# Even layer up to the output projection: the key norm's root pinned later, projections ahead of scores from the second key group on, other banks for the statistics

## The chip, the cores and the metric

The kernel runs on one core of one Trainium2 chip. Its time is the device time of one execution in microseconds (us). The figure for a kernel is the median of several executions. One further execution is taken with the hardware profiler; its spans, waits and chains are what the text argues from.

The engines are called as the profile calls them: PE is TensorE (matmul), PEld its weight loads, DVE is VectorE, ACT is ScalarE, POOL is GpSimd, and SP is the engine whose queue issues nearly all DMAs here. SBUF is the on-chip memory, PSUM the matmul's accumulation memory of eight banks.

## What is computed

The input is 1024 tokens of width 1024, with 16 meta tokens put ahead, so 1040 columns. Two layers follow. The first ("even") layer is the one that the change touches. Cut to what matters:

```python
def even_layer(z, w_in, ...):                       # z = rms_norm(h, norm_g[0])
    zp = jnp.einsum('btd,de->bte', z, w_in)
    c_q, c_kv, k_pe, q_s, k_s, v_s, gate = split_cols(zp, EVEN_SPLITS)   # 384, 256, 64, 1024, 256, 256, 2048
    y_a = mla_mixer(c_q, c_kv, k_pe, ...)           # 8 heads, full attention, low-rank q and kv
    y_b = swa_mixer(q_s, k_s, v_s, ...)             # 8 query heads, 2 key heads, window +-128 and the meta tokens, learned sink
    y = jnp.concatenate([y_a, y_b], axis=-1) * jax.nn.silu(gate)
    return jnp.einsum('bte,ed->btd', y, w_out)

def swa_mixer(q_s, k_s, v_s, g_qn, g_kn, sink, cos, sin):
    q = apply_rope(rms_norm(q, g_qn), cos, sin)     # 8 heads of 128
    k = apply_rope(rms_norm(k, g_kn), cos, sin)     # 2 heads of 128, each serves 4 query heads
    ...                                             # softmax over sink, 16 meta keys, 384 band keys; times v
```

The second ("odd") layer is a gated linear recurrence in both directions with its own projections; the change leaves it as it is. All products are of float32 accuracy: each operand is split into a high and a low part in a reduced format, and three matmuls (low by high, high by low, high by high) make one product.

## The kernel before

Activations lie transposed, 128 features on the partitions and the 1040 columns along the free axis; a projection of 128 output features is `proj1`. It has two halves of four 128-row pieces each; a half is 36 matmuls (4 pieces, 3 terms, 3 column chunks of `C3`: 348, 346, 346). Its weights come by a 256 KB load on SP's queue and are split into high and low on POOL (`split_w`, lines 106 and 107).

A Python program writes the work down in one order. A list scheduler then gives each engine its own queue: it takes instructions by priority (earlier in the program is higher, and weight loads are moved ahead), and if one is not ready by the scheduler's own reckoning it takes a later one that is. On the chip each queue is in order, so a queue that is ahead of the data simply waits. Every SBUF tile comes from a pool with a fixed number of buffers per tag (`T`, `S`, ...), every PSUM tile from a bank tag, and a new tile waits until a buffer is released.

The stages of the even layer that the change touches:

1. **Up projections** (lines 415 to 478). `uq_pair` makes three 128-row tiles of queries for two heads (the rope part first, j = 2, then j = 0 and 1), `uk_pair` two tiles of keys. `take` copies a tile out of PSUM in three chunks, on DVE or on ACT; `fold` squares it on ACT. The sums of squares over the partitions come from `stat`: POOL and DVE split the squares in two (lines 173 and 174), and the inner function `later` runs the matmuls against a column of ones and copies three chunks out on ACT (lines 188 and 189). `put_off(n, fn)` queues such a function; `tick()`, called once per finished tile, counts down and runs what has come due. PSUM has tags `b` (2 banks for each chunk) and `one` (2 banks).
2. **Window attention** (from line 515). PSUM tags: `b` 1 bank for each chunk, `s` 2, `t` 2, `a` 1. First `v_prep`, `k_prep(0)`, `q_prep(0)` and `gate_tile(0)` run. `k_prep(g)` projects the keys of key head g, starts the norm's statistic, and ropes the keys; `fin` (one tick later) runs the statistic and `row_rsqrt`: the row of sums goes to DRAM and comes back as a 16x65 tile, DVE takes the inverse root by three Newton steps (lines 126 to 132), and the result goes to DRAM again. `fin2` (two ticks later) reads it back broadcast to all partitions (`rkb`) and multiplies the keys by it (line 554). `put` splits the keys into `kh` and `kl` (lines 561 to 564). `q_prep` is alike for two query heads.
   Then 36 units follow, each two query heads by 128 queries (or the 16 meta queries, `i == 8`). A unit has `scores` (matmuls at line 684, softmax in place, last step line 703), `turn` (transposes, lines 718 and 721, tiles `tA` and `tB` of tag `t`, copied out at lines 723 to 732) and `values` (line 743, copied out as `yt`, stored to `s_yb`). Iteration c of the loop does `scores(c)`, `turn(c-1)`, `pull`, `values(c-2)`. `pull` advances a chain of the remaining projections (`q_prep(1)` to `gate_tile(9)`, 32 half-projection steps, each priced 5.3) by a credit of 4.6. Units 0 to 17 use key head 0, units 18 to 35 key head 1; at c = 18 `put` and `v_split` of key head 1 run first.
3. **The last gates** (line 822). `gate_tile(e, False)` for e = 10 to 15: projection, tanh, product (lines 766 to 769), and then `gated`: it loads the attention output `yb`, multiplies it by the gate on POOL (line 779) and splits it (lines 758 and 759). The tiles of e = 8 and 9, whose gates were stored earlier, are multiplied in the same loop. Tag `T` has 8 buffers here.
4. **The output projection's first half** (line 944) over `YH[8:16]`, with weights split on POOL again.

Of the kernel before, what the change touches and what calls it, by code (L numbers as in the profile page):

```python
# [7 lines left out]
F32 = mybir.dt.float32  # L8
# [9 lines left out]
T = 1040  # L18
# [23 lines left out]
def trunk_kernel(ctx: ExitStack, tc: tile.TileContext, a: dict, out: bass.AP):  # L42
# [126 lines left out]
    def stat(sq, s, m, dst, tag=None, rt="S"):  # L169

        hi = row("sqh", rt, F32R)
        lo = row("sql", rt, F32R)
        nc.gpsimd.tensor_scalar(hi, sq, 1.0, 1.0, ALU.mult, ALU.mult)
        nc.vector.tensor_sub(lo, sq, hi.bitcast(F32))

        def later():
            sr = row("sr", "T")
            if tag is None:
                ps = big("st")
                for j, x in enumerate((hi, lo)):  # L180
                    for c0, c1 in CH:
                        nc.tensor.matmul(ps[:m, OFF + c0:OFF + c1], s, x[:, c0:c1], start=j == 0, stop=j == 1)
                nc.scalar.copy(sr[:m], ps[:m, OFF:OFF + T])
            else:
                for c0, c1 in C3:
                    ps = bank("st", tag)
                    for j, x in enumerate((hi, lo)):
                        nc.tensor.matmul(ps[:m, :c1 - c0], s, x[:, c0:c1], start=j == 0, stop=j == 1)
                    nc.scalar.copy(sr[:m, c0:c1], ps[:m, :c1 - c0])
            nc.sync.dma_start(dst, sr[:m])  # L190

        return later
# [240 lines left out]
    def uq_pair(pr):  # L433
        for j in (2, 0, 1):
            ps = up_tile(a["uq"][pr * 3 + j], 3, cqh, cql)
            r = row("qr", "T")
            if j == 2:
                take(ps, r)
                t2 = row("qs2", "S")
                nc.scalar.activation(t2, r, AF.Square)  # L440
                rope(r, 32, tabC, tabS)
                nc.sync.dma_start(s_qr[pr], r)
                t0, t1 = row("qs0", "S"), row("qs1", "S")
            else:
                take(ps, r, True)
                fold(r, j, t0, t1)
                nc.sync.dma_start(s_qn[2 * pr + j], r)
        nc.vector.tensor_add(t0, t0, t2)
        nc.vector.tensor_add(t0, t0, t1)
        put_off(3, stat(t0, sel, 2, d_mq[pr], "one"))  # L450

    def uk_pair(pr):
        t0, t1 = row("ks0", "S"), row("ks1", "S")
# [4 lines left out]
            fold(r, j, t0, t1)  # L458
            nc.sync.dma_start(s_kn[2 * pr + j], r)
        nc.vector.tensor_add(t0, t0, t1)  # L460
        put_off(3, stat(t0, sel, 2, d_mk[2 * pr:2 * pr + 2], "one"))

    for pair, pr in ((uq_pair, 0), (uq_pair, 1), (uk_pair, 0), (uq_pair, 2), (uk_pair, 1), (uk_pair, 2), (uk_pair, 3),
                     (uq_pair, 3)):
# [72 lines left out]
    def k_prep(g):  # L537
# [7 lines left out]
        sk = stat(sq, one, 1, d_sk[g], "s")  # L545
        rope(raw, 64, sC, sS, eng=nc.gpsimd)

        def fin():
            sk()
            row_rsqrt(d_sk[g], 128, d_rks[g])  # L550

        def fin2():
            rkb = bcast_row(d_rks[g], "rkb", "T")
# [11 lines left out]
            KV[g, "k"] = (kh.rearrange("p b c -> p (b c)"), kl.rearrange("p b c -> p (b c)"))  # L565

        put_off(1, fin)
        put_off(2, fin2)
        KV[g, "put"] = put
        yield 5.3  # L570
# [184 lines left out]
    def split(src, nm, tag, w=T, eng=nc.vector):  # L755
# [3 lines left out]
        eng.tensor_sub(lo[:, :w], src[:, :w], hi[:, :w].bitcast(F32))  # L759
        return hi, lo  # L760

    def gate_tile(e, spill=True):
        o = []
        yield from steps(proj1(16 + e), o)
        g = row("gt", "T")
        evac(o[0], lambda t, c: nc.vector.scalar_tensor_tensor(g[:, c], t, 0.5, rstd[:, c], ALU.mult, ALU.mult))
# [3 lines left out]
        if spill:  # L770
            nc.sync.dma_start(s_gate[e], t)
        else:
            gated(e, t)
        yield 5.3

    def gated(e, t):
        y = row("yb", "T")
        nc.sync.dma_start(y, s_yb[e - 8])
        nc.gpsimd.tensor_mul(y, y, t)
        YH[e], YL[e] = split(y, "yb", "Y")  # L780

    def chain(*gs):
# [22 lines left out]
    for c in range(n + 2):  # L805
        if c < n:
            if units[c].i == 8:
                flush()
                if c == 18:
                    KV[1, "put"]()  # L810
                    v_split(1, None)
            units[c].scores()
        if 0 <= c - 1 < n:
            units[c - 1].turn()
        pull(jobs, PULL)
        if 0 <= c - 2 < n:
            units[c - 2].values()
    for _ in jobs:
# [4 lines left out]
    for e in range(8 + NX, 16):  # L823
        for _ in gate_tile(e, False):
            pass
        if e - 8 - NX < NX:
            t = row("gl", "T")
            nc.sync.dma_start(t, s_gate[e - NX])
            gated(e - NX, t)

    HD = {}
    LAG = 2.0
# [672 lines left out]
```

## Time and profile before

| what | value |
|---|---|
| median of 3 executions | 1940.13 us (1939.22 to 1945.82) |
| the profiled execution | 1936.07 us |
| its span, first to last instruction | 1934.3 us |
| mean granted TensorE clock | 0.986 of full |
| PE busy | 1828.5 us (95%) |
| DVE busy | 1278.4 us (66%) |
| POOL busy | 943.9 us (49%) |
| ACT busy | 827.9 us (43%) |
| stages: up projections | about 100 to 197 us of the span |
| window attention with projections | about 197 to 594 us |
| last gates | about 594 to 662 us |
| output projection, first half | from 666 us |

Times in the rows of a timeline are microseconds from the span's start. "idle before <-releaser" in brackets is the time that the engine had nothing to do before this instruction, and the instruction or DMA that ended it. Waits for PE are what costs time, as PE is busy nearly throughout; a wait of another engine matters only where PE comes to wait for what it was to make. In a row of stretches ("windows"), each engine has its busy time and count, then the granted TensorE clock, the DMA engines' busy share and GB/s.

### The profile page before, as it was taken

The numbers are of one execution on the slowest core, as the hardware profiler recorded it, in microseconds if no ns is written. First come the engines' busy times: TensorE is split into PE (matmuls) and PEld (weight loads), VectorE is DVE, ScalarE is ACT, GpSimd is POOL, SyncE is SP. The second block draws the span as 40 slices with busy tenths as digits, with TensorE's granted clock in tenths as the row PEclk, the third lists the DMA queues.
The fourth block names the chain that finished last, engine by engine and source line by source line (L and its number), as shares of the span: only waits on it lengthen the run. The fifth ranks groups of instructions, "written<-read, shape, count | busy, mean of one in ns | idle before, by whom it ended". The sixth has DMA issues, their size and how long they took to land.

```text
span 1934.3 us, 28455 instructions
## 1 busy us (share of the span) xinstructions
PE 1828.5 (95%) x10822; PEld 1659.4 (86%) x10822; DVE 1278.4 (66%) x1953; ACT 827.9 (43%) x1366; POOL 943.9 (49%) x780
## 2 busy tenths in 40 slices
PE   8999989998999999999999999999999899988999
PEld 7988988888999999788878999988888788876887
DVE  7686358787663432889888753368898989893000
ACT  5455224444342201666666642155656464652000
POOL 5455355535224652544433333358676777655331
PEclk9999999999999999999999999999999999998999
DMA  5256532222223451323221014312222222246521
GB/s 180 73 184 232 132 84 65 64 75 72 78 75 122 143 194 57 113 73 92 69 70 55 18 47 160 106 50 71 82 67 81 84 69 88 66 157 232 183 82 44
DMA packets 111062, 192.77 MB, mean 100 GB/s; under 512 B 32143, under 2 KB 51727, under 8 KB 110926
## 3 DMA queue, kind: packets, MB, share of 16 engines
q1 hardware_dynamic: 110926, 190.96, 31.4%
q8 instruction: 85, 1.39, 0.3%
q14 instruction: 51, 0.42, 0.1%
HBM read 129.86 MB, written 53.06 MB: 95 GB/s over the span
## 4 chain that ended last, share of the span: by engine, by line
PE 53%; DVE 20%; POOL 9%; issue 9%; DMA 5%; ACT 4%; SPq 1%; DVEq 0%; ACTq 0%; POOLq 0%
PE pj L159 10%; PE oo L159 8%; PE pxop L159 6%; PE px L918 4%; PE av L998 4%; PE op L159 3%; PE up L159 3%; PE tp L982 3%; PE vps L426 2%; DVE tz L1243 2%; DMA wr<-in_wg 2%; POOL oz L1253 2%; POOL wl L107 2%; DVE oxc L1167 2%; PE pg L1143 2%
## 5 line engine op out<-in xcount | busy, mean ns | idle before, releaser
L106 POOL TENSOR_SCALAR wh<-wr 128x512 fp32r<-128x512 f32 (+2 forms) x219 | 196.3, 897 | 396.4 <-PE pj L159 99.0
L107 POOL TENSOR_TENSOR wl<-wr,wh 128x512 fp32r<-128x512 f32 (+2 forms) x219 | 352.6, 1610 | 17.5
L159 PE MATMUL pj<-xh,wl 128*128 128x346 f32 (+1 forms) x768 | 251.8, 328 | 12.3 <-DVE wl L107 7.2
L159 PE MATMUL pj<-xl,wh 128*128 128x346 f32 (+1 forms) x768 | 249.3, 325 | 0.7 <-DVE xl L260 0.6
L159 PE MATMUL pj<-xh,wh 128*128 128x346 f32 (+1 forms) x768 | 248.9, 324 | 0.0
L159 PEld LDWEIGHTS pj<-xh,wl 128*128 128x128 f32 x768 | 146.6, 191 | 14.2 <-ACT xh L259 7.1
L159 PEld LDWEIGHTS pj<-xl,wh 128*128 128x128 f32 x768 | 146.7, 191 | 2.2 <-DVE xl L260 2.1
L159 PEld LDWEIGHTS pj<-xh,wh 128*128 128x128 f32 x768 | 146.6, 191 | 0.1
L936 POOL TENSOR_SCALAR mpm<-p,mmx 128x96 f32<-128x96 f32 (+1 forms) x69 | 25.7, 372 | 209.2 <-DVE mmx L931 119.9
L1143 PE MATMUL pu<-h1h,wl 128*128 128x346 f32 (+1 forms) x384 | 125.5, 327 | 0.8 <-POOL wh L106 0.8
L1143 PE MATMUL pu<-h1l,wh 128*128 128x346 f32 (+1 forms) x384 | 124.9, 325 | 0.0
L1143 PE MATMUL pu<-h1h,wh 128*128 128x346 f32 (+1 forms) x384 | 124.8, 325 | 0.0
L988 ACT CAST pth<-tp 128x512 fp32r<-128x512 f32 (+1 forms) x160 | 78.9, 506 | 83.4 <-PE tp L982 82.0
L1294 DVE TENSOR_TENSOR hres<-oo,hres 128x512 f32<-128x512 f32 x16 | 10.6, 687 | 151.6 <-PE oo L159 151.6
L989 DVE TENSOR_TENSOR ptl<-tp,pth 128x512 fp32r<-128x512 f32 (+1 forms) x160 | 91.9, 583 | 23.3 <-ACT pth L988 21.7
L159 PE MATMUL oo<-oyl,wh 128*128 128x512 f32 x256 | 102.3, 400 | 4.4 <-DMA oyl<-s_yl 4.4
L159 PE MATMUL oo<-oyh,wl 128*128 128x512 f32 x256 | 100.3, 401 | 3.3 <-DMA oyh<-s_y 3.3
L159 PE MATMUL oo<-oyh,wh 128*128 128x512 f32 x256 | 102.7, 402 | 0.0
L1143 PE MATMUL pg<-h1h,wl 128*128 128x512 f32 x256 | 101.4, 396 | 0.0
L1143 PE MATMUL pg<-h1h,wh 128*128 128x512 f32 x256 | 101.1, 395 | 0.0
L1143 PE MATMUL pg<-h1l,wh 128*128 128x512 f32 x256 | 100.8, 394 | 0.0
L982 PE MATMUL tp<-ident,p 128*128 128x128 f32 (+1 forms) x576 | 96.2, 274 | 0.0
(446 smaller groups left out, 5564.5 us busy)
## 6 DMA issues: line engine op xcount, KB each, us to landing
wr<-in_w SPq DMA_DIRECT2D x128, 256.0 KB
wr<-in_wo SPq DMA_DIRECT2D x64, 256.0 KB
s_y<-oyh SPq DMA_DIRECT2D x14, 512.0 KB
s_yl<-oyl SPq DMA_DIRECT2D x14, 512.0 KB
oyh<-s_y SPq DMA_DIRECT2D x14, 512.0 KB
oyl<-s_yl SPq DMA_DIRECT2D x14, 512.0 KB
s_g<-gth SPq DMA_DIRECT2D x10, 520.0 KB
xr<-in_x SPq DMA_DIRECT2D x8, 520.0 KB
```

The lines of the kernel that those rows point to most:

```text
L106: eng.tensor_scalar(hi[:, :n], raw[:, :n], 1.0, 1.0, ALU.mult, ALU.mult)
L107: eng.tensor_sub(lo[:, :n], raw[:, :n], hi[:, :n].bitcast(F32))
L159: nc.tensor.matmul(t[:, :c1 - c0], w, x[:, c0:c1], start=first and j == 0 and pi == 0, stop=last and j == nt - 1 and pi == 2)
L426: nc.tensor.matmul(ps[:m, :n], s, w, start=j == 0 and pi == 0, stop=j == nt - 1 and pi == 2)
L918: nc.tensor.matmul(dst[:m, d0:d0 + a1 - a0], l[:, s], r[:, a0:a1], start=pi == 0, stop=pi == 4)
L982: nc.tensor.transpose(tp[:, o:o + m], p_[:m, NM + P * (kt + j):NM + P * (kt + j) + P], ident[:m, :m])
L988: nc.scalar.copy(hi[:, :w], tp[:, :w])
L989: nc.vector.tensor_sub(lo[:, :w], tp[:, :w], hi[:, :w].bitcast(F32))
L998: nc.tensor.matmul(av[:, :n], l[:, vs], pts[kt][o][:, j * n:j * n + n], start=kt == 0 and j == 0 and pi == 0, stop=False)
L1143: nc.tensor.matmul(t[:, :c1 - c0], l, r[:, c0:c1], start=hf == 0 and k == 0 and pi == 0, stop=hf == 1 and k == 3 and pi == 2)
L1167: nc.vector.scalar_tensor_tensor(xc[:, 2:T], u[:, 0:T - 2], cw[0], xc[:, 2:T], ALU.mult, ALU.add)
L1243: nc.vector.scalar_tensor_tensor(tz[:, d, :n], av[:, :n], 1.0, tz[:, d, :n], ALU.add, ALU.mult)
```

## The change

Seven edits, all in the even layer up to the output projection:

- `stat` with tag `s` puts its third chunk into a bank of tag `t`.
- `uq_pair` copies the tile j = 1 out on ACT in place of DVE.
- The statistics of `uq_pair` and `uk_pair` are put off four ticks in place of three.
- In `k_prep`, `fin` only runs the statistic and loads the row back; the root and its store move to a new `fin1`, one tick later, just ahead of `fin2`. The root's first instruction is pinned behind the DVE instruction that was written last before it (an order on the queue, no wait for its result).
- In `gate_tile(e, False)` and for e = 8 and 9 the load of `yb` is written ahead of the projection (or of the product).
- The product `yb` times gate moves from POOL to DVE.
- From c = 18 on, `pull` comes ahead of `scores(c)`; iterations 36 and 37 keep it where it was.

```diff
@@ -182,8 +182,8 @@
                         nc.tensor.matmul(ps[:m, OFF + c0:OFF + c1], s, x[:, c0:c1], start=j == 0, stop=j == 1)
                 nc.scalar.copy(sr[:m], ps[:m, OFF:OFF + T])
             else:
-                for c0, c1 in C3:
-                    ps = bank("st", tag)
+                for c, (c0, c1) in enumerate(C3):
+                    ps = bank("st", "t" if tag == "s" and c == 2 else tag)
                     for j, x in enumerate((hi, lo)):
                         nc.tensor.matmul(ps[:m, :c1 - c0], s, x[:, c0:c1], start=j == 0, stop=j == 1)
                     nc.scalar.copy(sr[:m, c0:c1], ps[:m, :c1 - c0])
@@ -442,12 +442,12 @@
                 nc.sync.dma_start(s_qr[pr], r)
                 t0, t1 = row("qs0", "S"), row("qs1", "S")
             else:
-                take(ps, r, True)
+                take(ps, r, j == 0)
                 fold(r, j, t0, t1)
                 nc.sync.dma_start(s_qn[2 * pr + j], r)
         nc.vector.tensor_add(t0, t0, t2)
         nc.vector.tensor_add(t0, t0, t1)
-        put_off(3, stat(t0, sel, 2, d_mq[pr], "one"))
+        put_off(4, stat(t0, sel, 2, d_mq[pr], "one"))
 
     def uk_pair(pr):
         t0, t1 = row("ks0", "S"), row("ks1", "S")
@@ -458,7 +458,7 @@
             fold(r, j, t0, t1)
             nc.sync.dma_start(s_kn[2 * pr + j], r)
         nc.vector.tensor_add(t0, t0, t1)
-        put_off(3, stat(t0, sel, 2, d_mk[2 * pr:2 * pr + 2], "one"))
+        put_off(4, stat(t0, sel, 2, d_mk[2 * pr:2 * pr + 2], "one"))
 
     for pair, pr in ((uq_pair, 0), (uq_pair, 1), (uk_pair, 0), (uq_pair, 2), (uk_pair, 1), (uk_pair, 2), (uk_pair, 3),
                      (uq_pair, 3)):
@@ -545,9 +545,19 @@
         sk = stat(sq, one, 1, d_sk[g], "s")
         rope(raw, 64, sC, sS, eng=nc.gpsimd)
 
+        got = []
+
         def fin():
             sk()
-            row_rsqrt(d_sk[g], 128, d_rks[g])
+            t16 = small.tile([16, 65], F32, tag="t16", name="t16", bufs=2)
+            nc.sync.dma_start(t16, flat(d_sk[g]))
+            got.append(t16)
+
+        def fin1():
+            t16 = got[0]
+            tc.keep_in_program_order(nc.vector.scalar_tensor_tensor(t16, t16, 1.0 / 128, e16, ALU.mult, ALU.add))
+            y16 = newton_rsqrt(t16, [16, 65], "16")
+            nc.sync.dma_start(flat(d_rks[g]), y16)
 
         def fin2():
             rkb = bcast_row(d_rks[g], "rkb", "T")
@@ -565,6 +575,7 @@
             KV[g, "k"] = (kh.rearrange("p b c -> p (b c)"), kl.rearrange("p b c -> p (b c)"))
 
         put_off(1, fin)
+        put_off(2, fin1)
         put_off(2, fin2)
         KV[g, "put"] = put
         yield 5.3
@@ -759,8 +770,15 @@
         eng.tensor_sub(lo[:, :w], src[:, :w], hi[:, :w].bitcast(F32))
         return hi, lo
 
+    def y_in(e):
+        y = row("yb", "T")
+        nc.sync.dma_start(y, s_yb[e - 8])
+        return y
+
     def gate_tile(e, spill=True):
         o = []
+        if not spill:
+            y = y_in(e)
         yield from steps(proj1(16 + e), o)
         g = row("gt", "T")
         evac(o[0], lambda t, c: nc.vector.scalar_tensor_tensor(g[:, c], t, 0.5, rstd[:, c], ALU.mult, ALU.mult))
@@ -770,13 +788,11 @@
         if spill:
             nc.sync.dma_start(s_gate[e], t)
         else:
-            gated(e, t)
+            gated(e, t, y)
         yield 5.3
 
-    def gated(e, t):
-        y = row("yb", "T")
-        nc.sync.dma_start(y, s_yb[e - 8])
-        nc.gpsimd.tensor_mul(y, y, t)
+    def gated(e, t, y):
+        nc.vector.tensor_mul(y, y, t)
         YH[e], YL[e] = split(y, "yb", "Y")
 
     def chain(*gs):
@@ -809,10 +825,13 @@
                 if c == 18:
                     KV[1, "put"]()
                     v_split(1, None)
+            if c >= 18:
+                pull(jobs, PULL)
             units[c].scores()
         if 0 <= c - 1 < n:
             units[c - 1].turn()
-        pull(jobs, PULL)
+        if c < 18 or c >= n:
+            pull(jobs, PULL)
         if 0 <= c - 2 < n:
             units[c - 2].values()
     for _ in jobs:
@@ -826,7 +845,7 @@
         if e - 8 - NX < NX:
             t = row("gl", "T")
             nc.sync.dma_start(t, s_gate[e - NX])
-            gated(e - NX, t)
+            gated(e - NX, t, y_in(e - NX))
 
     HD = {}
     LAG = 2.0
```

## The prediction

> **What bounds the kernel.** I read the page's busy times first, then PE's waits up to 260 us and from 260 to 700 us (columns: total us, times, longest), then a row of stretches around the longest of them.
>
> ```profile
> PE 1828.5 (95%) x10822; PEld 1659.4 (86%) x10822; DVE 1278.4 (66%) x1953; ACT 827.9 (43%) x1366; POOL 943.9 (49%) x780
> ```
>
> ```profile
> PE st L188 <- DVE sql L174: 3.8, 3, 1.7
> ```
>
> ```profile
> PE tA L718 <- DVE sp L703: 7.3, 10, 1.6
> PE st L188 <- ACT sr L189: 6.0, 5, 1.9
> PE pj L159 <- ACT qraw L318: 3.9, 1, 3.9
> PE pxop L159 <- POOL wh L106: 3.2, 1, 3.2
> PE sps L684 <- DVE kl L564: 2.9, 1, 2.9
> PE sps L684 <- ACT kh L562: 1.1, 1, 1.1
> ```
>
> ```profile
> 248.00:282.00 34.00, 29.37 (x166) 27.73 (x165) 23.20 (x30) 12.15 (x21) 19.06 (x14) 0.90 0.30 81
> 436.00:450.00 14.00, 10.09 (x51) 9.71 (x50) 7.31 (x17) 5.38 (x12) 5.16 (x7) 0.76 0.36 104
> 594.00:662.00 68.00, 67.54 (x428) 67.54 (x429) 25.81 (x28) 12.80 (x14) 40.43 (x28) 1.00 0.34 117
> 662.00:672.00 10.00, 6.78 (x28) 6.53 (x27) 4.58 (x6) 2.72 (x3) 6.60 (x5) 0.66 0.73 243
> ```
>
> PE is busy for 95% of the span, so no other engine's work counts unless PE waits for it. All that the change can win lies in PE's idle time: 3.8 + 7.3 + 6.0 + 3.9 + 3.2 + 2.9 + 1.1 = 28.2 us in these rows, and the 7.3 us of transposes waiting for the softmax are not addressed by any edit. That leaves 20.9 us.
>
> The stretches show a second price. The granted clock is 0.90, 0.76 and 0.66 in the three that hold the three longest stops, and 1.00 in the one between. PE's timeline shows what that costs:
>
> ```profile
> 263.95 0.66 PE L159 MATMUL pj<-xh,wl 128*128 128x348 f32 x1 [3.93 <-ACT qraw L318]
> 268.94 0.32 PE L159 MATMUL pj<-xh,wh 128*128 128x346 f32 x1
> 269.89 0.32 PE L159 MATMUL pj<-xh,wh 128*128 128x346 f32 x1
> 666.02 0.63 PE L159 MATMUL pxop<-ybh,wl 128*128 128x348 f32 x1 [3.22 <-POOL wh L106]
> 671.63 0.32 PE L159 MATMUL pxop<-ybl,wh 128*128 128x346 f32 x1
> ```
>
> From 263.95 to 268.94 PE starts 17 matmuls, 0.29 us apart; from 268.94 to 269.89 six, 0.158 apart. At 0.158 the 17 would take 2.7 us, so the slow stretch costs 2.3 us. From 666.02 to 671.63 there are 19, 5.6 us for 3.0: it costs 2.6. The third stretch I price alike at 2.5, an estimate from these two. So the stops of 3.93, 1.1 + 2.9 and 3.22 us cost another 7.4 us together, and the whole that the edits can reach is 20.9 + 7.4 = 28.3 us.
>
> **The change part by part.** All positions are those of the profiled execution.
>
> *The root of key head 0.* DVE, then ACT:
>
> ```profile
> 254.28 0.22 DVE L313 SCALAR_TENSOR_TENSOR t<-t,e 16x65 f32<-16x65 f32 x1 [6.34 <-DMA t<-d_sk]
> 258.26 0.22 DVE L132 SCALAR_TENSOR_TENSOR nw_y<-nw_t,nw_y 16x65 f32<-16x65 f32 x1
> 258.40 1.22 DVE L398 TENSOR_TENSOR sw<-sw,sS 128x1040 f32<-128x1040 f32 x1
> 260.81 1.53 DVE L400 TENSOR_TENSOR qraw<-qraw,sw 128x1040 f32<-128x1040 f32 x1
> 262.38 1.06 ACT L624 CAST sqh__2740<-qraw 128x1040 fp32r<-128x1040 f32 x1 [10.95 <-DVE qraw L400]
> 263.45 1.14 ACT L318 COPY qraw<-pj 128x348 f32<-128x348 f32 x3
> ```
>
> DVE stood 6.34 us for the row that comes back from DRAM, then made the root (254.28 to 258.48, 4.2 us), then the query's rope (258.40 to 262.34, three operations, 3.9 us). ACT's split of that query waits for the rope and stands ahead of the next evacuation (263.45), for which PE waits until 263.95. With the root one tick later and pinned, the rope goes first. It can't start before its swapped copy has landed, which no row shows; the bounds are the 4.2 us of the root that leave its front plus the wait, and nothing. I take the middle of 0 and 4.2, some 2.2 us. PE's stop falls from 3.9 to 1.7 us, too short for a slow stretch by the rows seen here, so 2.2 + 2.3 = **4.5 us** (bounds 0 and 6.2). The root itself, the DRAM round trip and the split of the keys come later; they are covered by the gate's projection, 72 matmuls or 11.4 us. If that cover is too short, the first scores wait for the keys.
>
> *Statistics put off by four ticks; one copy on ACT.* The 3.8 us of `st L188 <- DVE sql L174` are three statistics whose low part DVE had not finished when PE came to them. One more tile of work (18 matmuls for keys, 27 for queries, so 2.8 us at least at 0.158) stands in between now, and the longest wait was 1.7. Three chunk copies for each of four query pairs leave DVE, the late engine, for ACT. Against it: the split squares stay in their buffers one tile longer, with six buffers of that tag, and a later fold may wait. I take **3.8 us** (bounds 1.5 and 4.5).
>
> *The third chunk in a bank of tag t.* The 6.0 us are the third chunk waiting for ACT to empty the first of only two banks.
>
> ```profile
> 410.84 0.68 DVE L727 TENSOR_TENSOR pl<-tA,ph 128x512 fp32r<-128x512 f32 x1
> 413.00 0.32 PE L188 MATMUL st<-sqh,ones 128*1 128x346 f32 x1 [1.90 <-ACT sr L189]
> ```
>
> At 413.00 the longest, 1.90 us. Its new bank holds the transposes that DVE reads until 410.84 + 0.68 = 411.52, so about 0.5 us of wait stay there, a gain of 1.4. The other 4.1 us go, but the next transposes find one of their two banks held until ACT's last chunk copy; for that I take off 1.5. Together **4.0 us** (bounds 1.5 and 6.0).
>
> *Projections ahead of scores.* In the steady state the order scores, turn, pull, values becomes pull, scores, turn, values. Between a unit's scores and its own turn lie one pull, one set of values and the next scores in both, so the 7.3 us stay. Two places differ. The first is unit 18:
>
> ```profile
> 425.15 0.22 DVE L132 SCALAR_TENSOR_TENSOR nw_y<-nw_t,nw_y 16x65 f32<-16x65 f32 x1
> 429.08 0.38 SPq L143 DMA_DIRECT2D rkb<-d_rks  x1
> 434.44 1.24 DVE L554 TENSOR_TENSOR kraw<-kraw,rkb 128x1040 f32<-128x1040 f32 x1 [2.44 <-DMA rkb<-d_rks]
> 435.78 0.42 DVE L732 TENSOR_TENSOR spmr<-tB,spmr 32x256 fp32r<-32x256 f32 x1
> 439.07 1.35 DVE L564 TENSOR_TENSOR kl<-kraw,kh 128x128 fp32r<-128x128 f32 x1
> ```
>
> Here the root ended at 425.37, the row was back on all partitions at 434.44, and the low keys were ready at 440.42; PE had stopped for 1.1 and 2.9 us. A half projection of 36 matmuls, 5.7 us, would now come first and hide it. But the root of this head moves as well. It is pinned behind the last instruction of the turn of unit 16, line 732, here at 435.78, or 433.3 without the 2.44 us of waiting just ahead of it. So it ends at 433.3 + 4.2 = 437.5. The round trip took 434.44 - 425.37 = 9.1 us here, 3.7 of them before SP issued the load at 429.08; with 8 us the row is back at 445.5, and 4 to 6 us later, at 449.5 to 451.5, the keys are ready. PE's two stops before 440.42 began at some 436.3, where the values of unit 15 ended; the step would run from there to 442.0. The root's store and the load back stand on SP's queue behind whatever weight load waits for POOL, which is how the 3.7 us came about. If the scores are next on its queue it stops for 8 us where it stopped for 4 (a loss of 4); if the scheduler fills with the turn, the values and the next step (2 + 5.7 us, to 449.7), almost nothing is left (a gain of 3.9 + 2.5 = 6.4). It fills by its own reckoning, and that reckoning took the keys for ready 4 us too early here. I take a stop of 3 us with its slow stretch: **1.0 us**.
>
> The second place is the end. The 32 steps run out at the 36th pull (36 x 4.6 / 5.3 = 31.2), which was the cover of the last softmax and now stands ahead of its scores:
>
> ```profile
> 581.83 0.30 PE L684 MATMUL sps<-kh,sqh__5194 128*128 128x288 f32 x1
> 582.75 0.41 PE L159 MATMUL pj<-xh,wl 128*128 128x348 f32 x1
> 588.52 0.28 PE L743 MATMUL av<-pl,svh 128*128 128x256 f32 x1
> 594.46 0.43 PE L159 MATMUL pj<-xh,wl 128*128 128x348 f32 x1 [0.74 <-ACT yt L746]
> 585.54 0.71 DVE L703 TENSOR_SCALAR sp<-sp,ssm 128x272 f32<-128x272 f32 x2
> 592.49 0.42 DVE L732 TENSOR_TENSOR spmr<-tB,spmr 32x256 fp32r<-32x256 f32 x1
> ```
>
> The last scores ended at 582.13 and the next stage began at 594.46, 12.3 us of which the step took 582.75 to 588.52, 5.8. Without it 6.6 remain. The softmax needs until 586.25, 4.1 us after the scores. The last turn and its copies took from about 589.7 (ten matmuls of values after 588.52) to 592.91, 3.2 us, and the last values with their copy 1.55. In a chain that is 4.1 + 3.2 + 1.55 = 8.9 us for 6.6: I take **-2.5 us** (bounds 0, if the next stage's projection could start sooner, which the wait for `yt` at 594.46 speaks against, and -5 with a slow stretch).
>
> *The last gates.* POOL splits the weights and also multiplied the tiles:
>
> ```profile
> L779 POOL TENSOR_TENSOR yb<-yb,gth 128x1040 f32<-128x1040 f32 x6 | 14.6, 2426 | 18.2 <-DVE gth L769 12.7 <-DMA yb<-s_yb 5.5
> L779 POOL TENSOR_TENSOR yb<-yb,gl 128x1040 f32<-128x1040 f32 x2 | 6.9, 3446 | 0.0
> L759 DVE TENSOR_TENSOR ybl<-yb,ybh 128x1040 fp32r<-128x1040 f32 x8 | 15.1, 1892 | 29.5 <-ACT ybh L758 29.5
> ```
>
> Eight products, 14.6 + 6.9 = 21.5 us, leave POOL, which was busy 40 of 68 us. The last splits for the output projection were queued behind the product of tile 14 and came 3.22 us late. DVE takes over eight operations like its line 759, at most 1.9 us each, 15 us; it was busy 25.8 of 68 us, and the product now follows the gate on the same engine with no POOL between. The loads of `yb` are issued sooner on SP's queue. If POOL was the last to be late, 3.2 + 2.6 = **5.8 us** (bounds 2 and 5.8).
>
> The sum is 4.5 + 3.8 + 4.0 + 1.0 - 2.5 + 5.8 = 16.6 us. The profiled execution took 1936.07, so its like takes 1919.5. The median was 4.1 us above it, at 1940.13, so I say **1923.5**.
>
> The slow stretches have a page. The Trainium skill, "TensorE: Matmul & The Clock Gate", section "HAM oscillation — how this bites in real kernels", says that the clock falls back after idle gaps of over some 3.4 us. Here stops of 3.22 us, and of 3.14 in a stage not touched, were followed by a lower clock too, so the trace draws the line lower:
>
> ```profile
> 974.77 0.38 PE L918 MATMUL py<-knh,qnl 128*128 128x256 f32 x1 [3.14 <-ACT p L928]
> ```
>
> By the page's figure a stop of 3 us at unit 18 would keep full speed, and the sum would be 19.1 us; by the rows it may lose it, as I have counted.
>
> **The rivals.** *The waits come back elsewhere.* In-order queues that were late for one reason are late for the next: DVE stands for the key rows ahead of the softmaxes (the row at 434.44 shows such a stand), unit 18 stops for 8 us (-4 for +1, 5 us less) and the bank swap is paid back in the turns (4 us less). That leaves 7.6 us, 1932.5 by the median. For it: the 7.3 us of softmax waits show how little slack DVE has. Against it: DVE's load falls.
>
> *All of it is covered.* Unit 18 has its keys in time (+6.4) and the tail costs nothing: 16.6 + 5.4 + 2.5 = 24.5 us, 1915.6.
>
> *The other side: the load of `yb` holds up SP's queue.* It stands ahead of a projection's weights, takes one of eight `T` buffers, and if none is free all weights behind it wait until the tile before is split. The price per tile is what late weights cost at 666.02, 3.22 + 2.6 = 5.8 us; six tiles are 35 us against the other parts' 10.8 us, so 1964. It decides from the second such tile on. Against it: a tile needs three buffers at a time, five where a stored gate is loaded, and weight loads have their own priority ahead.
>
> **How the numbers follow.** The forecast, gains of 11 to 24 us, has 0.53; covered in full 0.11; the waits come back 0.24; SP's queue 0.05; the other 0.07 is a schedule that shifts in later stages, split between same and slower. What a measurement of this kernel can tell from no change is about 0.5%, 9.7 us either way. All of the first two, 0.64, is faster; the third is just under 9.7 and goes to same, with 0.03 of the rest: 0.27; slower 0.09. The range runs from 1910 (the bounds of all terms, 28 us) to 1938 (the returned waits with the tail at its worst, and the scatter of the runs).
>
> **What would show it.** In the changed profile: no waits of `st` for `sql` before 160 us; waits of `st` for `sr` under 2 us in all; the stop at some 260 us under 2 us and the clock 1.00 up to 430 us; a stop of 2 to 4 us ahead of the scores of unit 18; 2 to 3 us more idle around the last turn; no stop ahead of the first `pxop`, and POOL's busy time 21 us lower with DVE's some 10 to 15 higher. The forecast is wrong if PE's idle time up to 680 us falls by under 8 us, or if a new stop of over 4 us appears there.

## The result, and the profile after

The changed kernel is slower: 1959.44 us median (1949.19 to 1962.53) against 1939.84 us for the kernel before on the same chip, a ratio of 1.0095 with a 95% interval of 1.0074 to 1.0116. The forecast was 1923.5 us, range 1910 to 1938. The profiled execution took 1959.94 us, its span 1958.1, 23.8 us more than before. By the medians it is 19.6 us: the profiled execution of the kernel before was 3.8 us under its median.

Engine totals of the changed kernel, then its PE waits up to 260 us, then those from 260 to 700 us (columns: total us, times, longest):

```profile
PE 1836.9 (94%) x10822; PEld 1665.0 (85%) x10822; DVE 1285.5 (66%) x1949; ACT 832.9 (43%) x1378; POOL 922.6 (47%) x772
```

```profile
PE st L188 <- ACT sr L189: 2.1, 3, 0.9
PE st L188 <- DVE sql L174: 2.0, 1, 2.0
PE up L159 <- DVE kr L318: 1.3, 1, 1.3
```

```profile
PE st L188 <- DVE sql L174: 8.7, 1, 8.7
PE tA L729 <- DVE sp L714: 8.0, 12, 1.6
PE sps L695 <- DVE qm L638: 4.7, 1, 4.7
PE sps L695 <- ACT kh L572: 3.1, 1, 3.1
PE sps L695 <- ACT sr L189: 2.6, 3, 1.4
PE sps L695 <- DVE kl L574: 2.4, 1, 2.4
PE pj L159 <- ACT qraw L318: 2.4, 1, 2.4
...
PE pxop L159 <- POOL wh L106: 0.8, 1, 0.8
```

The waits that the edits aimed at did shrink (`pj` for `qraw` 3.9 to 2.4, `pxop` 3.2 to 0.8, the 6.0 us of `st` for `sr` in the attention gone). But there are two new ones of 8.7 and 4.7 us, and they hang on DVE. Where the 23.8 us arose, from the first matmul of each stage in PE's timeline:

| first matmul of | before, us | after, us | behind |
|---|---|---|---|
| values' projection | 197.46 | 200.57 | 3.1 |
| first scores | 281.97 | 292.53 | 10.6 |
| scores of unit 9 | 356.92 | 371.48 | 14.6 |
| projections behind the attention | 594.46 | 614.73 | 20.3 |
| output projection (`pxop`) | 666.02 | 687.18 | 21.2 |
| end of the span | 1934.3 | 1958.1 | 23.8 |

The largest steps are the first scores (7.5 us), the stretch from unit 9 to the projections behind the attention (5.7 us) and the nine units behind the first scores (4.0 us). The last of these goes with a slow clock, as the rows of stretches show, whose last three numbers are the granted clock, the share of DMA and GB/s: 0.96 from 282 to 436 us, where before it was 1.00. Cut finer it is 0.75 from 292 to 300 us, right behind the two stops, and 1.00 from 300 us on. 0.94 and 0.92 stand at the two ends of the table, ahead of the values' projection and behind the attention.

```profile
110.00:170.00 60.00, 54.99 (x328) 51.15 (x327) 40.19 (x50) 38.92 (x55) 36.66 (x34) 0.94 0.53 182
248.00:282.00 34.00, 26.23 (x163) 24.80 (x162) 15.22 (x19) 8.64 (x15) 18.14 (x15) 1.00 0.30 76
282.00:436.00 154.00, 135.48 (x864) 127.06 (x864) 116.14 (x275) 67.31 (x180) 68.50 (x71) 0.96 0.25 62
594.00:662.00 68.00, 64.49 (x393) 63.15 (x392) 36.12 (x58) 16.89 (x32) 22.89 (x22) 0.92 0.32 107
```

How the two stops came about is read from DVE's timeline and SP's of the changed kernel (start, duration, and in brackets the idle time before with what ended it):

```profile
260.50 1.24 DVE L398 TENSOR_TENSOR sw<-sw,sS 128x1040 f32<-128x1040 f32 x1 [9.59 <-DMA sw<-qraw]
...
267.10 0.21 DVE L558 SCALAR_TENSOR_TENSOR t<-t,e 16x65 f32<-16x65 f32 x1
...
274.07 1.35 DVE L132 SCALAR_TENSOR_TENSOR nw_y<-nw_t,nw_y 16x65 f32<-16x65 f32 x1
281.41 1.24 DVE L564 TENSOR_TENSOR kraw<-kraw,rkb 128x1040 f32<-128x1040 f32 x1 [5.99 <-DMA rkb<-d_rks]
...
284.91 1.23 DVE L174 TENSOR_TENSOR sql<-qs,sqh 128x1040 fp32r<-128x1040 f32 x1
...
286.26 1.24 DVE L398 TENSOR_TENSOR sw<-sw,sS 128x1040 f32<-128x1040 f32 x1
...
292.21 0.17 DVE L638 TENSOR_TENSOR qm<-qraw,qm 128x16 fp32r<-128x16 f32 x1
```

```profile
275.45 0.33 SPq L560 DMA_DIRECT2D d_rks<-nw_y  x1
276.80 0.33 SPq L143 DMA_DIRECT2D rkb<-d_rks  x1
277.23 0.47 SPq L396 DMA_DIRECT2D sw<-qraw  x1
```

DVE's first rope operation had to wait 9.59 us for the swapped copy, and the pinned root behind it began at 267.10 in place of 254.28, though the load of its row had been issued at 255.57 (in the kernel before DVE began the root 2.1 us after that issue). It took 8.3 us (to 275.42) where it took 4.2. SP stood 9.1 us for the root (the row of its waits says `SPq L560 <- DVE nw_y L132: 9.1, 1, 9.1`) and could issue the second query's swap only behind it, at 277.23. DVE then stood 5.99 us for the row of roots, and behind that stood the low part `sql` of the query's squares, for which PE stopped 8.67 us, and the second query's rope and split, for which it stopped 4.73 us.

### The profile page after: what moved, and what is told of

The parts are those of the page before. It is cut to its first block, busy times and chain, and to the rows that moved or that the text cites. A ratio compares the mean times of both kernels' runs of the same rounds, so it can differ in the third digit from the quotient of the medians.

```text
span 1958.1 us, 28468 instructions
## 1 busy us (share of the span) xinstructions
PE 1836.9 (94%) x10822; PEld 1665.0 (85%) x10822; DVE 1285.5 (66%) x1949; ACT 832.9 (43%) x1378; POOL 922.6 (47%) x772
## 4 chain that ended last, share of the span: by engine, by line
PE 48%; DVE 16%; POOL 6%; issue 5%; DMA 3%; ACT 3%; SPq 0%; DVEq 0%; ACTq 0%; POOLq 0%
PE pj L159 9%; PE oo L159 8%; PE pxop L159 6%; PE px L937 4%; PE av L1017 4%; PE op L159 3%; PE tp L1001 3%; PE pg L1162 3%; PE pu L1162 2%; DVE tz L1262 2%; DMA wr<-in_wg 2%; PE py L937 2%; POOL oz L1272 2%; DVE oxc L1186 1%; POOL wown L107 1%
## 5 line engine op out<-in xcount | busy, mean ns | idle before, releaser
L1313 DVE TENSOR_TENSOR hres<-oo,hres 128x512 f32<-128x512 f32 x16 | 10.6, 688 | 153.0 <-PE oo L159 153.0
L1008 DVE TENSOR_TENSOR ptl<-tp,pth 128x512 fp32r<-128x512 f32 (+1 forms) x160 | 92.0, 584 | 23.6 <-ACT pth L1007 21.8
```

The lines of the kernel that those rows point to most:

```text
L1008: nc.vector.tensor_sub(lo[:, :w], tp[:, :w], hi[:, :w].bitcast(F32))
```

## The experiments

Ratios are to the kernel before on the same chip, with 95% intervals.

**The root alone, put back and added.** In the changed kernel the root goes back, as below; in the kernel before the root alone moves, by the same lines the other way.

```diff
             sk()
+            row_rsqrt(d_sk[g], 128, d_rks[g])
...
-        put_off(2, fin1)
```

> The changed kernel with the first part taken back: the root of both key heads is made one tick earlier again, without the pin; the other four parts stay. Theory 1 (the late root of key head 0 stands in DVE's and SP's queues, and PE stops 8.7 + 4.7 us for it): these two stops go, the old stop of some 3.9 us at 260 us comes back, and the first scores come 8 to 11 us sooner, at 282 to 285 us; with the slow clock behind the stops the time falls by 10 to 16 us, to 1943 to 1949. Theory 2 (the order of projections and scores is what lengthens the attention): first scores sooner, but the stretch from there to the gates stays some 11 us longer than before, and the time falls by under 5 us. Theory 3 (the stages are shifted against each other and any edit costs): no change within 4 us.

> The kernel before with the first part alone: the root of the key heads one tick later and pinned. Theory 1: PE stops 10 to 14 us ahead of the first scores, which come at 290 to 294 us, and the time is 10 to 16 us above that of before, 1950 to 1956. Theory 2: the first scores come up to 3 us sooner or later, and the time is within 5 us of before. Theory 3: somewhat slower, 1943 to 1948, with no stop of over 5 us ahead of the first scores.

Measured: 1940.0 us, 1.0002 (0.9985 to 1.0018), first scores at 285.45; and 1954.91 us, 1.0064 (1.0046 to 1.0081), first scores at 289.77. Taking the root back won 19.4 us, more than the 10 to 16 expected, and the move alone cost 14.5. In the second run PE stopped 7.16 us for `sql` and 4.29 at the third chunk of that statistic, at nearly the same place as the changed kernel. The root is the loss. The other four parts together come out at nothing, where 12.1 us were forecast for them.

**The order put back.**

```diff
-            if c >= 18:
-                pull(jobs, PULL)
...
-        if c < 18 or c >= n:
-            pull(jobs, PULL)
+        pull(jobs, PULL)
```

> The changed kernel with the order of projections and scores from unit 18 on put back. Theory 1: the stops ahead of the first scores stay (13 us), unit 18 stops for 4 to 8 us, the tail is 2 to 3 us shorter, and the time is within 4 us of the changed kernel, 1955 to 1963. Theory 2: the time falls by 8 to 14 us, to 1946 to 1951, nearly all of it between unit 18 and the gates. Theory 3: no change within 4 us, but other stops in other places.

Measured: 1951.27 us, 1.0045 (1.0028 to 1.0061). It won 8.2 us, the lower end of what theory 2 expected: the order costs as well, beside the root. The stops ahead of the first scores stayed at 6.99 and 4.72 us; 5.0 us of the gain arose before the projections behind the attention (609.77 for 614.73).

**The pin taken away.** The root is one tick later in the program, but free.

```diff
-            tc.keep_in_program_order(nc.vector.scalar_tensor_tensor(t16, ...))
+            nc.vector.scalar_tensor_tensor(t16, ...)
```

> The changed kernel without the pin: the root is still made one tick later in the program's order, but the planner may put it wherever it thinks the data ready. Theory 1: if the pin is what makes the root late, it starts at some 261 us again ahead of the query's rope, the stops ahead of the first scores fall under 6 us, and the time is 1945 to 1950; if the tick is, the root stays at some 267 us and the time within 3 us of the changed kernel. Theory 2 and 3: within 3 us of the changed kernel in any case.

Measured: 1937.63 us, 0.9989 (0.9977 to 1.0001). DVE's timeline without the pin:

```profile
256.89 0.22 DVE L558 SCALAR_TENSOR_TENSOR t<-t,e 16x65 f32<-16x65 f32 x1 [6.28 <-DMA t<-d_sk]
...
261.17 1.22 DVE L398 TENSOR_TENSOR sw<-sw,sS 128x1040 f32<-128x1040 f32 x1
```

The scheduler put the root ahead of the rope again, ten microseconds sooner, and the whole loss went (21.8 us, more than theory 1 expected). The tick without the pin costs nothing; with the pin it is the change's loss.

**The other parts one by one**, each in the kernel before.

```diff
+                take(ps, r, j == 0)              # stage 1: copy on ACT, and
+        put_off(4, stat(...))                    # four ticks
...
+        nc.vector.tensor_mul(y, y, t)            # gates: product on DVE, load ahead
...
+                    ps = bank("st", "t" if tag == "s" and c == 2 else tag)   # banks
...
+            if c >= 18: pull(jobs, PULL)         # order: ahead of the scores
```

> The kernel before with the statistics of the latent's pairs put off by four ticks and one copy of each query pair on ACT, and nothing else. With the root as before the changed kernel still reached the values' projection 3.3 us late (200.8 us for 197.5), with two stops of 1.96 and 1.30 us close together at 142 to 144 us and a slow clock behind them. Theory 1 (this part made the two stops: one tick more lets the splits pile up behind each other): projection of values at 200 to 201 us, 0.94 clock from 110 to 170 us, time 1941 to 1945. Theory 2 (the third chunk's bank made them): projection at 196 to 198 us, waits of st for sql gone, time 1934 to 1939.

> The kernel before with the last gates' products on DVE and the loads of yb ahead of their projections, and nothing else. Theory 1 (this part did what was forecast and its gain was eaten elsewhere): no stop of over 1 us ahead of the first pxop, clock 1.00 from 662 to 672 us, POOL some 21 us less busy; the first pxop 4 to 6 us sooner and the time 3 to 7 us lower, 1933 to 1937. Theory 2 (the later stages give it back): the first pxop sooner by the same, and the time within 2 us of before.

> The kernel before with the third chunk of a statistic in a bank of tag t, and nothing else. Theory 1 (it removes ACT's waits and gives part of them back in the turns): waits of st for sr under 2 us in all up to 700 us, the first pxop 1 to 4 us sooner, time 1936 to 1940. Theory 2 (it is what delays the stages ahead of the attention): projection of the values at 200 us or later, and the time 2 to 4 us above before.

> The kernel before with the half projections ahead of the scores from unit 18 on, and nothing else. The root is as early as it was. Theory 1 (the order costs only where the keys are late): the stop of 1.1 + 2.9 us at unit 18 falls under 1 us and the clock stays 1.00 there, a gain of 4 to 6 us, and the end of the attention loses 1 to 4 us: time 1934 to 1941. Theory 2 (the order is a loss by itself, as putting it back in the changed kernel won 8 us): the stretch from unit 18 to the gates is 5 us or more longer than before, net of the one projection that comes ahead of it, and the time is 1943 to 1950.

| part alone | us | ratio | forecast, us | by the median, us |
|---|---|---|---|---|
| stage 1 | 1940.28 | 1.0001 (0.9989 to 1.0013) | -3.8 | +1.4 |
| gates | 1934.87 | 0.9985 (0.9973 to 0.9998) | -5.8 | -4.0 |
| banks | 1940.96 | 1.0010 (1.0000 to 1.0020) | -4.0 | +2.1 |
| order | 1943.67 | 1.0030 (1.0020 to 1.0040) | +1.5 | +4.8 |
| root (from above) | 1954.91 | 1.0064 (1.0046 to 1.0081) | -4.5 | +14.5 |

The last column sums to 18.8 us, and the whole change cost 19.6. That they agree so well is partly luck, since the parts aren't independent: the four without the root sum to +4.3 us alone and came out at -0.4 together, and the order cost 4.8 us alone but 8.2 in the changed kernel. A single entry of 1 to 2 us is within the scatter of the runs. Of the theories, the first held for stage 1 in its two stops (the time came out just under its range) and for the gates, and the second for the order. For the banks the first held in its mechanism and not in its gain: the first `pxop` came only 0.1 us sooner, and the time was 1 us above its range.

*Stage 1.* Two of PE's stops in the profile of this part, and the stretch around them:

```profile
141.88 0.48 PE L188 MATMUL st<-sql,sel 128*2 128x348 f32 x2 [1.95 <-DVE sql L174]
143.66 0.66 PE L159 MATMUL up<-ckh,wl 128*128 128x346 f32 x1 [1.30 <-DVE kr L318]
```

```profile
140.00:150.00 10.00, 6.82 (x24) 6.43 (x25) 7.50 (x13) 5.05 (x6) 5.96 (x6) 0.66 0.52 191
```

Three waits for `sql` became one, but a copy of `kr` now stands behind that split and a rope operation on DVE, and the two stops lie 0.5 us apart. The clock fell to 0.66, PE started 24 matmuls in that stretch for 46 before, and the values' projection began at 200.80 us for 197.46. Most of it was won back at unit 18, where the keys were late less (at 442.68 a stop of 2.50 and no second of over 1 us): the delay fell from 3.8 us at unit 17 to 1.1 at unit 19. *Banks.* The waits of `st` for `sr` in the attention fell from 6.0 to nothing, as forecast, and these rows of its waits from 260 to 600 us show where they went:

```profile
PE sps L684 <- DVE smx L685: 2.0, 2, 1.6
PE tA L718 <- DVE nw_t L130: 1.7, 1, 1.7
PE pj L159 <- DVE gt L766: 1.5, 1, 1.5
...
PE sps L684 <- ACT sr L189: 1.2, 2, 0.7
PE st L188 <- DVE pl L727: 1.1, 1, 1.1
```

They sum to 7.5 us. Before, the rows of the same names were 1.2, 0.8, 0.2, nothing and nothing, 2.2 us: 5.3 returned for 6.0 removed. *Gates.* Its wait at `pxop` fell from 3.2 to 0.8 and its clock was 1.00 from 662 to 672 us for 0.66; DVE's product took 1.24 to 1.65 us. *Order.* Unit 18 no longer stops (no wait of `sps` for `kh` or `kl` is left), but its first softmax does, and the end of the attention stops twice close together:

```profile
453.94 0.28 PE L718 MATMUL tA<-ident,sp 32*128 32x32 f32 x1 [2.72 <-DVE sp L703]
...
589.42 0.36 PE L743 MATMUL av<-pl,svh 128*128 128x256 f32 x1 [1.22 <-ACT sp L694]
593.73 0.58 PE L743 MATMUL av<-pl,svh 128*128 128x256 f32 x1 [1.40 <-DVE pl L727]
```

```profile
580.00:600.00 20.00, 16.48 (x94) 15.41 (x94) 9.28 (x24) 6.19 (x18) 3.25 (x6) 0.84 0.23 77
```

**The pin on one key head, and DVE without its stand.**

```diff
+            if g: tc.keep_in_program_order(ins)      # pin on the second key head only
...
+        if g: put_off(2, fin2)                       # key head 0 reads no row of roots back
```

> The changed kernel with the pin on the root of the second key head alone; the root of key head 0 is free to go ahead of the query's rope. Theory 1a (the pin costs at key head 0, where DVE, SP and PE have nothing else to do): first scores at 284 to 286 us, time within 4 us of the changed kernel without any pin, 1934 to 1942. Theory 1b (the pin costs at both): first scores at 284 to 286 us, a stop of over 4 us ahead of unit 18, and 1943 to 1950.

> The changed kernel, in which the keys of key head 0 are not multiplied by their root: the root is made and stored as late as before, but its row is not read back, and DVE does not stand for it. Left out is one product of 128x1040 and one load. Theory 1c (DVE's stand of 6 us at the row is what PE's stops come from): the stop of 8.7 us falls under 2 us and that of 4.7 us under 2; first scores at 282 to 286 us, time 1940 to 1947. Theory 1d (SP's queue is: the root's store keeps it for 9 us, and the second query's loads stand behind it): the second query's swap still ends no sooner than 284 us, a stop of 4 us or more stays ahead of the first scores, which come at 287 us or later; time 1948 to 1956.

Measured: 1945.78 us, 1.0027 (1.0017 to 1.0037); and 1948.55 us, 1.0048 (1.0033 to 1.0064). The pin on the second key head costs 8.1 us against none: 4.6 between the first scores and unit 18, where PE stops 3.29 + 1.58 us, but 3.5 ahead of the first scores, where nothing of it runs; there DVE came to the gate's first product 1.6 us later than without any pin (283.47 for 281.87, in the same order), and PE stopped 4.09 us for it instead of 1.45. The rows show how DVE came to be later: the rope's last two operations took 1.64 and 2.19 us, ending 1.1 us behind one of POOL's two weight splits each (these ended at 280.23 and 282.45), where they took 1.23 and 1.53 without any pin. POOL's first split began 1.0 us sooner there (279.08 for 280.12), as PE had freed its buffers sooner. No pinned instruction is in this chain, so whether these 3.5 us belong to the pin stays open; first scores at 284 to 286 us were expected and came at 288.25, and the time and the stop at unit 18 are those of theory 1b. Pinning key head 0 too costs another 13.7.

The second run leaves out one load and one product of the keys. Without the row's return the stop of 8.67 us became 3.20, that of 4.73 went, one of 1.13 for the gate's first product came, and the time fell by 10.9 of those 13.7 us. That is less than theory 1c expected (first scores by 286 us and 1940 to 1947 us; they came at 288.69, and the time was 1948.55). What hangs on the row's return is thus most of the loss, but the run doesn't part it: with DVE's stand, the split of the keys behind the row and the second query's late swap went too. The 3.20 us are `sql` behind the root itself, which took from 270.02 to 279.55. So SP's part wasn't told apart: its queue had the second query's swap ahead of the root's store in this run (271.26 and 279.57, where the changed kernel issued the swap at 277.23), and theory 1d was not put to the test.

**What the old stop at 264 us was.** The forecast's first term took it for ACT's split of the query. The first run here has the gates' part and one more half projection ahead of unit 18, the second also puts that split behind ACT's emptying of the banks.

```diff
+                    pull(jobs, 5.3)                            # at c == 18, both runs
+        pull(jobs, PULL if c < 18 else 4.3)
...
+            for x in held:                                     # second run: the split of the
+                q_split(*x)                                    # first query behind the take
```

> The kernel before with the last gates' part of the change, and one half projection more ahead of the scores of unit 18 (the pulls after it are made smaller, so that the last softmax keeps its cover); the order is otherwise the old one. Theory 1 (the order lost only at the end of the attention): unit 18 stops for under 1.5 us, the stretch from the last scores to the next stage is no longer than the 12.6 us of before, and the time is 1929 to 1933. Theory 2 (the order is a loss by itself): 1935 to 1940.

> As the run with the gates and one half projection more ahead of unit 18, and in addition the split of the first query comes behind ACT's emptying of the second query's banks. The stop of 3.9 us at 264 us was put down to the root of key head 0; if it comes from the split, which stands ahead of that emptying on ACT and waits for the rope, it falls under 1 us and its slow clock goes, with the root where it was. The first scores come 2 to 5 us sooner than in that run, and the time is 2 to 5 us lower. If the stop comes from elsewhere, both are as they were within 1 us.

Measured: 1938.56 us, 0.9994 (0.9983 to 1.0004); and 1939.52 us, 0.9997 (0.9988 to 1.0007). The extra projection brought nothing: unit 18 no longer stopped, but its softmax did (2.35 us at 452.58) and a later statistic (1.75 at 473.33). In the second run the emptying was first on ACT, and the stop was still 3.45 us:

```profile
262.81 1.15 ACT L318 COPY qraw<-pj 128x348 f32<-128x348 f32 x3 [11.39 <-DVE qraw L400]
263.98 1.06 ACT L619 CAST sqh__2836<-qraw 128x1040 fp32r<-128x1040 f32 x1
```

ACT stood for the rope's last operation with an instruction that doesn't read its result. So it was the destination: tag `T` has four buffers, and the keys, the first query, its swapped copy and the row of roots hold them until line 400 is done with the copy. The run without the row's return agrees: there no row of roots takes a buffer and the keys are split early, and ACT began to empty the second query's banks at 262.32, when only PE had kept it waiting, ahead of line 400 (265.42). The next runs give the swapped copies of the first pair a buffer of the queries' tag; the second has the gates' part beside it, the third the banks too.

```diff
-            rope(raw, 64, sC, sS, eng=...)
+            rope(raw, 64, sC, sS, "q" if u == 0 else "T", eng=...)
```

> The kernel before, in which the swapped copies of the first pair of queries lie in a buffer of the query's tag (six, of which four are in use then) and not in one of the four of tag T; nothing else. Theory B (ACT's emptying waits for a free buffer of tag T, which the rope's last operation releases): the stop of 3.9 to 4.4 us at 264 us falls under 1 us and the clock stays 1.00 there, with the root where it was; the first scores come 0 to 4 us sooner (the second query's rope stands close behind), and the time falls by 1 to 6 us, to 1934 to 1939. Theory S (the split or the root holds ACT): the stop stays over 3 us and the time within 1.5 us of before.

> As the run before it, and in addition the last gates' part of the change. Theory B: the two gains add up, 1930 to 1935. Theory S: as the last gates' part alone, 1934 to 1937.

> As the run before it, and in addition the third chunk in a bank of tag t. Alone that part removed the waits of st for sr and brought nothing (1.001, 1.000 to 1.002), so it is expected to bring nothing here: within 2 us of the run without it.

Measured: 1941.59 us, 1.0014 (1.0003 to 1.0025); 1935.84 us, 0.9992 (0.9982 to 1.0002); 1936.11 us, 0.9990 (0.9979 to 1.0001). ACT's timeline, PE's and a stretch of the first of them:

```profile
256.35 0.45 ACT L318 COPY qraw<-pj 128x348 f32<-128x348 f32 x1 [4.72 <-PE pj L159]
```

```profile
273.61 0.32 PE L188 MATMUL st<-sql,sel 128*2 128x348 f32 x1 [1.35 <-DVE sql L174]
279.10 0.66 PE L159 MATMUL pj<-xh,wl 128*128 128x348 f32 x1 [3.87 <-DVE gt L766]
```

```profile
270.00:290.00 20.00, 14.12 (x72) 12.33 (x71) 16.91 (x31) 3.39 (x7) 9.27 (x7) 0.74 0.25 68
```

The stop at 264 is gone, with the root where it was: theory B is right about its cause. It was wrong about the gain, for this run and for the next (the banks brought nothing again, as expected): 15 us later PE stops for 3.87 us, the first scores come at 285.16 for 281.97, and the kernel is no faster. The stop moves, because DVE sets when PE can go on. It came to the gate's first product at 278.54 us for 278.80 before, so the matmul that waits for it began at 279.10 for 279.36, though PE was there some 4 us sooner. Between 270 and 290 us DVE is busy for 16.91 of 20 us, for 13.96 before.

The lowest median of all has the kernel before with the gates' part alone, 1934.87 us. Its interval ends at 0.9998, so it beats the kernel before by little, and the changed kernel by 24.6 us.

## Why the prediction was wrong

Gains count as positive here, as in the prediction. *The root of key head 0* (+4.5, bounds 0 and 6.2; alone -14.5 by the medians). This is the step that failed, and in two places. The gain was argued from the wrong wait: "ACT's split of that query waits for the rope and stands ahead of the next evacuation". The order on ACT was read rightly, but the cause was a buffer of tag `T`; a profile shows which instruction freed PE, and not whether it was read, overwritten or merely queued behind. The rope began 0.7 us sooner with the root alone (257.70 for 258.40), not 2.2, since its swapped copy landed only then, and PE's stop fell from 3.93 to 2.90 us, where 1.7 were forecast. And the loss had no lower bound: "covered by the gate's projection, 72 matmuls or 11.4 us. If that cover is too short, the first scores wait for the keys", with no price. The chain was there to be added up: the root 4.2 us, a round trip of some 6 (5.99 above), the keys' product and splits. What the pin queued the root behind (the swapped copy that DVE awaits, the rope, the query's split) made it start 10.0 us later with the root alone moved (264.31 for 254.28), and behind the root then stood `sql`, the second rope and SP's queue. That wait was named for the second key head and not for the first.

*Unit 18* (stop of 3 us forecast, +1.0). The stop was 3.13 + 2.41 us. The mechanism was the one told: in the changed kernel the pinned root began at 447.87, was stored at 452.22, and DVE stood for its row:

```profile
451.97 0.22 DVE L132 SCALAR_TENSOR_TENSOR nw_y<-nw_t,nw_y 16x65 f32<-16x65 f32 x1
...
458.95 1.31 DVE L564 TENSOR_TENSOR kraw<-kraw,rkb 128x1040 f32<-128x1040 f32 x1 [5.59 <-DMA rkb<-d_rks]
461.37 3.45 DVE L573 TENSOR_TENSOR kl<-kraw,kh 128x1024 fp32r<-128x1024 f32 x1 [1.11 <-ACT kh L571]
```

The times were reckoned well: units 9 and 17 both stood 14.6 us behind, and less these the root began at 433.3 and the low keys were ready at 450.5, where 433.3 and 449.5 to 451.5 were reckoned (the round trip was 6.8 us for 8). What was mis-sized is how much of this the scheduler covers: 5.5 us of stop were left, where 3 were taken. *The tail* (-2.5, bounds 0 and -5): with the order alone 9.95 us lay between the last scores' end (586.15) and the next stage (596.10), 3.4 more than the 6.6 that were left, and another 1.9 us were lost from there to `pxop`, behind two stops of 1.22 and 1.40 with the clock at 0.84. So the lower bound was the right one. The slow clock was allowed for only as a bound.

*Statistics put off* (+3.8): the waits for `sql` fell as told (with this part alone from 3.8 us to 2.0), but those of `st` for `sr` up to 260 us rose from 0.2 to 2.3, and a later split of `sql` was counted as free for the copies queued behind it. *Banks* (+4.0): right in what it removes, wrong in taking off 1.5 for the turns; 5.3 came back. That is the rival in which "the waits come back elsewhere"; it held for these two parts. *Gates* (+5.8, bounds 2 and 5.8): right in kind, 4.0 by the medians, 0.4 to 5.2 by the interval of the ratio. In the changed kernel POOL was 21.3 us less busy, as told, and DVE 7.1 more, where 10 to 15 were told: its other loads fell.

The rival on the slower side was the queue of SP behind the load of `yb`, at 1964 us. It named nearly the right time for a reason that didn't occur: the gates alone were the one gain. SP's queue did hold up work, but behind the root's store. The signs listed for a wrong forecast (a new stop of over 4 us up to 680 us) are what the profile shows.

## What to carry to other kernels

An in-order pin on a late instruction is priced by all that waits behind it: write down for each engine and each DMA queue the next three instructions after the pinned one and who needs them, and add up the longest chain before calling it covered. When PE waits for a copy, ask whether that copy waited for its source, its place in the queue or its destination buffer; moving the source helps only in the first case. And where another engine sets the pace of a stretch, as DVE did here ahead of the first scores, a stop of PE that is taken out can come back a few microseconds later, so a sum over PE's waits is an upper bound of the gain.

## What was not expected of the hardware

*Small operations of DVE beside POOL.* The twelve operations of the root took 4.2 us in one place and 8.3 and 9.5 in others. In the changed kernel the DVE rows of two of them and the POOL row beside them:

```profile
268.28 0.22 DVE L132 SCALAR_TENSOR_TENSOR nw_y<-nw_t,nw_y 16x65 f32<-16x65 f32 x1
...
269.94 2.38 DVE L132 SCALAR_TENSOR_TENSOR nw_y<-nw_t,nw_y 16x65 f32<-16x65 f32 x1
```

```profile
269.80 2.44 POOL L643 TENSOR_TENSOR qs<-qs,qs 128x1040 f32<-128x1040 f32 x1
```

The same operation took 0.22 us alone and 2.38 while POOL added two full rows, and it ended 0.08 us after that addition. The Trainium skill, "SBUF — State Buffer", section "SBUF: two separate sides", says that VectorE operations with two inputs from SBUF and GpSimd share a pair of ports under an exclusive lock, so that the later one stands until the earlier is done; this pair of rows agrees. A move of a chain of small operations thus also changes which of POOL's operations stand beside it; here that made the root some 4 us longer, which no term had.

*The clock behind two short stops.* Stops of 1.95 and 1.30 us, 0.5 us apart, were followed by a clock of 0.66 in their stretch, and 1.22 and 1.40 us, 2.9 us apart, by 0.84, with no stop of 3 us near. Not every such pair does it: in the kernel before, 1.01 and 1.58 us, 4.4 us apart, left the clock at 1.00 from 344 to 354 us, and a lone stop of 2.38 us in the changed kernel left it at 1.00 from 248 to 282 us. What else decides wasn't tried.
